# Seven tiny loads on the scalar queue during the last store of a top-2 dispatch kernel

## The chip, the cores and the metric

The kernel runs on one core of a Trainium2 chip. The metric is device time in microseconds (us): the median of several executions. A single profiled execution is shown beside it, because its trace is what can be read. The core has a vector engine (VectorE, DVE in the profile), a scalar engine (ScalarE, ACT), GpSimd (POOL), a matrix engine (TensorE, PE, which has no work here), a sync engine (SyncE, SP) that issues most transfers, and 16 DMA engines that carry the transfers out.

## The reference, cut to what matters

The inputs are `x` with 16 x 1024 tokens of 512 float32 values, and `router_logits` with 8 float32 values for each token. For each token the two largest of the 8 logits are turned into two weights that add up to one, and the token's row of `x` is written out twice, once times each weight.

```python
probs = softmax(router_logits)                     # 8 experts
topk_indices = np.argsort(probs, axis=-1)[..., -k:]  # k = 2, smaller one first
topk_probs = np.take_along_axis(probs, topk_indices, axis=-1)
topk_probs = topk_probs / np.sum(topk_probs, axis=-1, keepdims=True)
x_expanded = x[:, :, np.newaxis, :].repeat(k, axis=2)
return (x_expanded * topk_probs[..., np.newaxis]).astype(np.float32)
```

The output, 16 x 1024 x 2 x 512 float32, is twice the size of `x`. The profile counts 34.08 MB read and 67.11 MB written.

## The kernel before, in words

**Tiling.** The 16,384 tokens are cut into two groups (`GROUPS`, line 42): 65 x 128 tokens, then 63 x 128. In each group every one of the 128 partitions of SBUF holds 65 (or 63) tokens that follow each other in memory, so a transfer of n tokens per partition is 128 long rows, one for each partition. `xs` (line 93) holds a whole group of `x`, `osp` (line 94) is a second buffer of 18 tokens' outputs.

**The weights.** All logits are loaded at the start by two transfers (lines 130 and 131) into a corner of `osp`. `top2_weights` (line 14) finds the two largest by a tournament of maxima and minima on VectorE, and two sigmoids on ScalarE (lines 37 and 38) give the weights `WA`.

**Loads, products, stores.** For each group, `LOADS` (line 44) lists the load sizes in tokens per partition, issued at line 122 on the sync queue, and `STORES` (line 47) lists the stores. For each store VectorE makes the products (line 138), in `osp` or back into parts of `xs` that are no longer needed, and one transfer writes them out (line 151). All stores go over the sync queue but the very first (3 tokens per partition), which goes over the scalar queue (line 149). The stores of the second group are 16, 16, 15 and 16 tokens per partition; the last one is 64 KB for each partition, 8 MB in all.

**The order.** `keep_in_program_order` fixes the order of the transfers on their queue as the loops write it. The list `moved` collects the loads of `x` and all stores in that order, so `moved[-1]` is the last store and `moved[-2]` the one before it. Waits are set by the framework: whoever reads or overwrites a buffer waits for the semaphore of whoever wrote or read it. Eight semaphores go round among the transfers.

**The end.** At line 155 the sync engine gets an empty instruction, `seen`, that waits for the weights, the last product and all transfers of `moved` but the last. What is left for the program's end (line 195 in the profile) is then the wait for the last store alone, and a barrier of all engines.

Of the kernel before, what the change touches and what calls it, by code (L numbers as in the profile page):

```python
# [1 line left out]

# [4 lines left out]

F32 = mybir.dt.float32
ALU = mybir.AluOpType
ACTF = mybir.ActivationFunctionType  # L10
P = 128


def top2_weights(nc, WA, dlt, room, logits, E):

    tt = nc.vector.tensor_tensor
    hi, lo, n = None, None, E  # L20
    while n > 1:
        n //= 2
        if hi is None:
            a, b = logits[:, :, 0:n], logits[:, :, n : 2 * n]
            nhi, nlo = room(n), b
            tt(nhi, a, b, op=ALU.max)  # L26
            tt(nlo, a, b, op=ALU.min)  # L27
        else:
            a, b = hi[:, :, 0:n], hi[:, :, n : 2 * n]
            nhi, nlo, tmp = room(n), room(n), room(n)  # L30
            tt(tmp, lo[:, :, 0:n], lo[:, :, n : 2 * n], op=ALU.max)  # L31
            tt(nlo, a, b, op=ALU.min)  # L32
            tt(nlo, nlo, tmp, op=ALU.max)  # L33
            tt(nhi, a, b, op=ALU.max)  # L34
        hi, lo = nhi, nlo
    tt(dlt, hi[:, :, 0], lo[:, :, 0], op=ALU.subtract)  # L36
    nc.scalar.activation(WA[:, :, 0], dlt, ACTF.Sigmoid, scale=-1.0)  # L37
    return nc.scalar.activation(WA[:, :, 1], dlt, ACTF.Sigmoid, scale=1.0)  # L38

GROUPS = [65, 63]

LOADS = [[2, 4, 28, 31], [16, 16, 31]]
BASE = [0, 1]

STORES = [
    [(0, 3, "osp", 0), (3, 15, "osp", 3), (18, 16, "xs", 0), (34, 15, "osp", 0), (49, 16, "xs", 33)],
    [(0, 16, "osp", 2), (16, 16, "xs", 0), (32, 15, "osp", 0), (47, 16, "xs", 32)],
]  # L50

L = 18

FREE = [3, 2]


@with_exitstack
def kernel(
    ctx: ExitStack,
    tc: tile.TileContext,  # L60
    x: bass.AP,
    router_logits: bass.AP,
    k: bass.AP,
    out: bass.AP,
):
    nc = tc.nc
    B, S, D = x.shape
    E = router_logits.shape[-1]
    N = B * S
    assert int(k) == 2 and E == 8 and N == P * sum(GROUPS)  # L70
    M = N // P

    x_v, o_v, rl_v = [], [], []
    t0 = 0
    for n in GROUPS:
        t1 = t0 + P * n
        x_v.append(
            x.rearrange("b s d -> (b s) d")[t0:t1].rearrange("(p m) d -> p m d", p=P)
        )
        o_v.append(  # L80
            out.rearrange("b s k d -> (b s) k d")[t0:t1].rearrange(
                "(p m) k d -> p m k d", p=P
            )
        )
        rl_v.append(
            router_logits.rearrange("b s e -> (b s) e")[t0:t1].rearrange(
                "(p m) e -> p m e", p=P
            )
        )
        t0 = t1  # L90

    wpool = ctx.enter_context(tc.tile_pool(name="wpool", bufs=1))
    xs = wpool.tile([P, max(GROUPS), D], F32)
    osp = wpool.tile([P, L, 2, D], F32)
    WA = wpool.tile([P, M, 2], F32)
    dlt = wpool.tile([P, M], F32)


    flat = osp.rearrange("p l k d -> p (l k d)")
    taken = [0]  # L100

    def room(n):
        o = taken[0]
        taken[0] += M * n
        return flat[:, o : o + M * n].rearrange("p (m n) -> p m n", n=n)

    logits = room(E)

    def place(where, at, n):

        if where == "osp":
            return osp[:, at : at + n]
        return xs[:, at : at + 2 * n, :].rearrange("p (r k) d -> p r k d", k=2)

    moved = []
    m0 = 0
    for g, G in enumerate(GROUPS):
        x0, r = BASE[g], 0
        for n in LOADS[g]:
            moved.append(  # L120
                tc.keep_in_program_order(
                    nc.sync.dma_start(  # L122
                        xs[:, x0 + r : x0 + r + n, :], x_v[g][:, r : r + n, :]
                    )
                )
            )
            r += n
            if g == 0 and r == 6:
                n0 = GROUPS[0]
                tc.keep_in_program_order(nc.sync.dma_start(logits[:, :n0], rl_v[0]))  # L130
                tc.keep_in_program_order(nc.sync.dma_start(logits[:, n0:], rl_v[1]))  # L131
                weights = top2_weights(nc, WA, dlt, room, logits, E)
        assert r == G
        for r, n, where, at in STORES[g]:
            og = place(where, at, n)
            again = where == "osp" and at == 0 and r > 0
            for a, b in [(0, FREE[g]), (FREE[g], n)] if again else [(0, n)]:
                product = nc.vector.tensor_tensor(  # L138
                    og[:, a:b],
                    xs[:, x0 + r + a : x0 + r + b, :]  # L140
                    .unsqueeze(2)
                    .to_broadcast([P, b - a, 2, D]),
                    WA[:, m0 + r + a : m0 + r + b, :]
                    .unsqueeze(3)
                    .to_broadcast([P, b - a, 2, D]),
                    op=ALU.mult,
                )

            queue = nc.scalar if g == r == 0 else nc.sync
            moved.append(  # L150
                tc.keep_in_program_order(queue.dma_start(o_v[g][:, r : r + n], og))  # L151
            )
        m0 += G

    seen = tc.keep_in_program_order(nc.sync.nop())
    for ins in [weights, product] + moved[:-1]:
        tc.add_manual_dep(
            seen.ins,
            ins.ins.name,
            mybir.DependencyInfo(  # L160
                mybir.DependencyClass.Sync, mybir.DependencyReason.DATA
            ),
            reason="all but the last transfer is done",
        )


# [1 line left out]
_INS = ['x', 'router_logits', 'k']  # L168
_OUTS = [((16, 1024, 2, 512), 'float32')]

_NUMBERS = {'k': 2}


# [26 lines left out]
```

## Time and profile before

| what | value |
|---|---|
| median of 3 runs | 239.66 us (239.65 to 239.67) |
| profiled execution, its own time | 241.36 us |
| span of its trace, first to last instruction | 239.6 us |
| VectorE busy | 141.9 us (59% of the span), 22 instructions |
| ScalarE busy | 1.8 us, 3 instructions |
| data moved | 101.19 MB in 2592 packets, 422 GB/s over the span |

The span is what the profiler recorded between the first and the last instruction; the time of the same execution, 241.36 us, has what lies around the span in it, 1.8 us here. A transfer is recorded twice: as an instruction of the queue that issues it (SPq for sync, ACTq for scalar) and as packets on the 16 DMA engines. Queue q1 is the sync engine's, q10 the scalar engine's. A packet here is one contiguous row of a transfer, or the 4 bytes with which a DMA engine reports on a semaphore that its part is done. The view of a window tells how many packets began in it, and the sum of their durations as a share of 16 engines over the window; a packet that begins in a window counts in full, so the share can be over 100%.

### The profile page before, as it was taken

How to read it: one execution, taken by the hardware profiler on the slowest of the kernel's cores; microseconds unless marked ns; L12 is line 12 of the kernel's file. 1: busy time of each engine (PE TensorE's matmuls, PEld its weight loads, DVE VectorE, ACT ScalarE, POOL GpSimd, SP SyncE). 2: the span in 40 equal slices, each digit the busy share in tenths (PEclk: the TensorE clock that was granted, in tenths of full speed). 3: DMA queues.
4: the chain of work that ended last, by engine and by line, in shares of the span. 5: the costliest groups of instructions: out<-in, count | busy, mean ns of one | idle time of the engine just before them, and what ended most of it. 6: DMA issues, size and time to landing. Idle time of an engine off the chain costs nothing.

```text
span 239.6 us, 106 instructions
## 1 busy us (share of the span) xinstructions
DVE 141.9 (59%) x22; ACT 1.8 (1%) x3; POOL 0.2 (0%) x4
## 2 busy tenths in 40 slices
DVE  0560499999789999200000699999405999960000
ACT  2000000000000000000000000000000000000000
POOL 0000000000000000000000000000000000000000
DMA  7989998979989897999899999999999899898984
GB/s 253 528 373 483 427 415 376 493 339 492 481 372 492 383 482 339 482 437 449 361 421 438 438 438 498 435 419 471 405 405 471 372 503 442 380 492 360 514 350 186
DMA packets 2592, 101.19 MB, mean 422 GB/s; under 512 B 288, under 2 KB 416, under 8 KB 672
## 3 DMA queue, kind: packets, MB, share of 16 engines
q1 hardware_dynamic: 2448, 99.62, 96.7%
q10 hardware_dynamic: 144, 1.57, 1.5%
HBM read 34.08 MB, written 67.11 MB: 422 GB/s over the span
## 4 chain that ended last, share of the span: by engine, by line
DMA 48%; DVE 40%; SPq 1%; issue 0%; DVEq 0%
DMA xs<-in_x_dram 25%; DVE osp L138 25%; DMA out_dram<-osp 23%; DVE xs L138 14%; SPq L122 0%; SPq L131 0%; SPq L130 0%; SPq L151 0%; DVEq L138 0%
## 5 line engine op out<-in xcount | busy, mean ns | idle before, releaser
L138 DVE TENSOR_TENSOR osp<-xs,WA 128x3072 f32<-128x3072 f32 (+5 forms) x7 | 69.4, 9909 | 62.7 <-DMA xs<-in_x_dram 47.3
L138 DVE TENSOR_TENSOR xs<-xs,WA 128x16384 f32<-128x16384 f32 x4 | 68.9, 17224 | 0.1
L26 DVE TENSOR_TENSOR osp<-osp 128x512 f32<-128x512 f32 x1 | 0.7, 693 | 8.5 <-DMA osp<-in_router_logits_dram 8.5
L37 ACT ACT_TABLE_LOAD x1 | 1.3, 1283 | 0.7 <-PEq L181 0.7
L27 DVE TENSOR_TENSOR osp<-osp 128x512 f32<-128x512 f32 x1 | 0.7, 691 | 0.0
L32 DVE TENSOR_TENSOR osp<-osp 128x256 f32<-128x256 f32 (+1 forms) x2 | 0.7, 351 | 0.0
L31 DVE TENSOR_TENSOR osp<-osp 128x256 f32<-128x256 f32 (+1 forms) x2 | 0.7, 350 | 0.0
L34 DVE TENSOR_TENSOR osp<-osp 128x256 f32<-128x256 f32 (+1 forms) x2 | 0.7, 350 | 0.0
L33 DVE TENSOR_TENSOR osp<-osp 128x256 f32<-128x256 f32 (+1 forms) x2 | 0.7, 350 | 0.0
L37 ACT ACTIVATE WA<-dlt 128x128 f32<-128x128 f32 x1 | 0.3, 315 | 10.5 <-DVE dlt L36 10.5
L36 DVE TENSOR_TENSOR dlt<-osp 128x128 f32<-128x128 f32 x1 | 0.3, 292 | 0.0
L38 ACT ACTIVATE WA<-dlt 128x128 f32<-128x128 f32 x1 | 0.3, 297 | 0.0
L181 POOL MEMSET const-bfloat16-1.0<- 128x1 bf16 x1 | 0.1, 101 | 0.0
L181 POOL MEMSET const-uint8-127<- 128x1 uint8 x1 | 0.1, 101 | 0.0
L181 POOL MEMSET const-float32-0.0<- 128x1 f32 x1 | 0.1, 98 | 0.2 <-issue 0.2
L181 POOL MEMSET const-float32-1.0<- 128x1 f32 x1 | 0.1, 98 | 0.0
## 6 DMA issues: line engine op xcount, KB each, us to landing
out_dram<-osp SPq DMA_DIRECT2D x3, 7680.0 KB, 23.5
xs<-in_x_dram SPq DMA_DIRECT2D x2, 7936.0 KB, 42.2
xs<-in_x_dram SPq DMA_DIRECT2D x2, 4096.0 KB, 40.1
xs<-in_x_dram SPq DMA_DIRECT2D x1, 7168.0 KB, 24.8
out_dram<-osp ACTq DMA_DIRECT2D x1, 1536.0 KB, 26.6
xs<-in_x_dram SPq DMA_DIRECT2D x1, 1024.0 KB, 5.9
xs<-in_x_dram SPq DMA_DIRECT2D x1, 512.0 KB, 3.9
osp<-in_router_logits_dram SPq DMA_DIRECT2D x1, 260.0 KB, 6.2
```

Of the source, the lines that this page charges most:

```text
L26: tt(nhi, a, b, op=ALU.max)
L27: tt(nlo, a, b, op=ALU.min)
L31: tt(tmp, lo[:, :, 0:n], lo[:, :, n : 2 * n], op=ALU.max)
L32: tt(nlo, a, b, op=ALU.min)
L33: tt(nlo, nlo, tmp, op=ALU.max)
L34: tt(nhi, a, b, op=ALU.max)
L36: tt(dlt, hi[:, :, 0], lo[:, :, 0], op=ALU.subtract)
L37: nc.scalar.activation(WA[:, :, 0], dlt, ACTF.Sigmoid, scale=-1.0)
L38: return nc.scalar.activation(WA[:, :, 1], dlt, ACTF.Sigmoid, scale=1.0)
L138: product = nc.vector.tensor_tensor(og[:, a:b], xs[:, x0 + r + a : x0 + r + b, :] .unsqueeze(2) .to_broadcast([P, b - a, 2, D]), WA[:, m0 ...
L181: nc = _bacc.Bacc("TRN2", target_bir_lowering=False, num_devices=1)
```

## The change

Behind the two groups' loops, seven small loads are issued on the scalar queue. Load i takes n rows, n = 2, 4, 6, 8, 10, 12, 14, each of 16 + i float32 values (64 to 88 bytes), from the logits into a buffer `marks` that nothing reads. Each is made to wait for `moved[-2]`, the last store but one. They are put at the front of `moved`, so that `seen` waits for them too. The rest of the hunk only gives the dependency a name (`done`).

```diff
+ENGINES = [2, 4, 6, 8, 10, 12, 14]
...
+    marks = wpool.tile([P, len(ENGINES), 16 + len(ENGINES)], F32)
...
+    done = mybir.DependencyInfo(mybir.DependencyClass.Sync, mybir.DependencyReason.DATA)
+    rows = router_logits.rearrange("b s e -> (b s) e").rearrange("(p m) e -> p (m e)", p=P)
+    last = moved[-2]
+    for i, n in enumerate(ENGINES):
+        small = tc.keep_in_program_order(
+            nc.scalar.dma_start(marks[:n, i, : 16 + i], rows[:n, : 16 + i])
+        )
+        tc.add_manual_dep(small.ins, last.ins.name, done, reason="late in the program")
+        moved.insert(0, small)
+
     seen = tc.keep_in_program_order(nc.sync.nop())
     for ins in [weights, product] + moved[:-1]:
         tc.add_manual_dep(
-            seen.ins,
-            ins.ins.name,
-            mybir.DependencyInfo(
-                mybir.DependencyClass.Sync, mybir.DependencyReason.DATA
-            ),
-            reason="all but the last transfer is done",
+            seen.ins, ins.ins.name, done, reason="all but the last transfer is done"
         )
```

In the built program the instructions of all engines but ACT are the same as before, in the same order. ACT has the seven transfers behind its one store; the first six of them wait for semaphores of earlier transfers (the first for two, one of them that of `moved[-2]`), the seventh for none of its own. The names and sizes of the waits of `seen` are unchanged, only the counts that it waits for are higher.

## The prediction

> **What bounds the kernel now.** I read the queues first, then the chain, then the waits of the sync engine, and last the packets in windows at the end. The page's queue part and the chain of waits (start, duration, what, in us):
>
> ```profile
> DMA packets 2592, 101.19 MB, mean 422 GB/s; under 512 B 288, under 2 KB 416, under 8 KB 672
> q1 hardware_dynamic: 2448, 99.62, 96.7%
> q10 hardware_dynamic: 144, 1.57, 1.5%
> ...
> 150.83 31.23 DMA out_dram<-osp
> ...
> 196.15 17.23 DVE xs L138
> ```
>
> The packets fill 96.7 + 1.5 = 98.2% of what 16 engines have in the span: the DMA engines bound the kernel, and whatever adds engine time adds to the end. The packets count out: the 18 transfers have 128 rows each, 18 x (128 + 16) = 2592, and 18 x 16 = 288 are under 512 B. So a transfer puts 8 rows and one tiny packet, its report to a semaphore, on each engine. The tail is the last store. In order of time from the sync queue, its waits (total, times, longest) and the instructions of lines 155 and 195 (ns min/median/max, first and last start):
>
> ```profile
> 213.40 0.33 SPq L151 DMA_DIRECT2D out_dram<-xs  x1
> ...
> out_dram<-xs SPq DMA_DIRECT2D x1, 25.4
> ...
> SPq L195 <- DMA out_dram<-xs: 19.2, 1, 19.2
> SPq L155 <- DMA out_dram<-osp: 5.5, 1, 5.5
> ...
> L155 SPq EVENT_SEMAPHORE  x5: 17/28/5505, 213.8 to 214.0; - x5
> ...
> L195 SPq DRAIN  x3: 7/7/7, 238.8 to 239.1; - x3
> ...
> L195 SPq COMPARE_BRANCH  x1: 33/33/33, 219.6 to 219.6; - x1
> ```
>
> The last store is issued at 213.40 and lands 25.4 later, at 238.8, where the closing drain starts; 0.8 us of barrier follow to 239.6. `seen` at L155 starts the last of its five waits at 214.0 and is held 5.5 us, to 219.5: that is when the last store but one has landed, and when the seven loads may go. Now the end itself, by packets that began in three windows, 236.3 to 237, 236.96 to 238.4, and 238.4 to 239:
>
> ```profile
> DMA packets 15, 0.00 MB, mean 0 GB/s; under 512 B 15, under 2 KB 15, under 8 KB 15
> ...
> q1 hardware_dynamic: 15, 0.00, 1.2%
> ```
>
> ```profile
> DMA packets 0, 0.00 MB, mean 0 GB/s; under 512 B 0, under 2 KB 0, under 8 KB 0
> ```
>
> ```profile
> DMA packets 1, 0.00 MB, mean 0 GB/s; under 512 B 1, under 2 KB 1, under 8 KB 1
> ```
>
> Fifteen engines report by 236.96, the sixteenth after 238.4. So one engine alone sets the end, at least 1.44 us behind the rest. An engine that is not this one has 1.44 us to give away; the late one has nothing. The trace doesn't number the engines, so it doesn't say which of them is late. The 15 reports took 1.2% of 16 x 0.7 us, 0.13 us, or 9 ns each.
>
> **The change part by part.** *Nothing is removed.* Up to 219.5 us no engine has a new instruction, so all before stands as it is, and the 8 MB of the last store are issued at 213.40 as before.
>
> *Issue.* ACT gets seven transfers. Its one transfer before and its one wait:
>
> ```profile
> L151 ACTq EVENT_SEMAPHORE  x1: 38/38/38, 12.5 to 12.5; - x1
> L151 ACTq DMA_DIRECT2D out_dram<-osp x1: 367/367/367, 16.4 to 16.4; - x1
> ```
>
> Seven times 0.37 is 2.6 us, and a few waits of 0.04: ACT issues from 219.5 to about 222.3 and then goes to the closing barrier, which it needs only at 238.8. Queued behind the waiting ACT are only its own seven loads and the barrier. Cover 16.5 us; cost nothing.
>
> *How the packets mix.* Queue q10 has run beside q1 once, with the first store. The window 16.4 to 43:
>
> ```profile
> DMA packets 320, 11.43 MB, mean 430 GB/s; under 512 B 32, under 2 KB 32, under 8 KB 32
> ...
> q1 hardware_dynamic: 176, 9.86, 87.3%
> q10 hardware_dynamic: 144, 1.57, 13.9%
> ...
> out_dram<-osp ACTq DMA_DIRECT2D x1, 1536.0 KB, 26.6
> ```
>
> 1.5 MB took 26.6 us to land although their packets are 13.9% of the engines' time: 9 packets an engine on q10, 11 on q1, about one for one. The shares add to 101.2%, so the mixing itself lost no engine time. I take from it that an engine serves one packet of each queue in turn. Beside the last store a turn is long. The window 221.7 to 236 has only its rows:
>
> ```profile
> DMA packets 95, 6.23 MB, mean 435 GB/s; under 512 B 0, under 2 KB 0, under 8 KB 0
> ...
> q1 hardware_dynamic: 95, 6.23, 100.4%
> ```
>
> 100.4% of 16 x 14.3 us over 95 packets is 2.42 us each. Between about 220.5 and 237 that gives 6 or 7 turns, so 6 or 7 tiny packets an engine slip between rows of the store, and what is left of an engine's tiny packets runs when its store is done. How many an engine gets no row shows for fewer than 128 rows. As 128 rows give 8 to each of 16, I take at most one row per load, so at most 7 rows and 7 reports, 14 packets; the other end is all 56 rows and 7 reports on one engine, 63.
>
> *Price of a tiny packet.* A report of 4 B took 9 ns. The next larger rows are those of the logits, window 7.1 to 7.3, and for the two large rows that also began in it, window 11.5 to 13:
>
> ```profile
> DMA packets 46, 0.20 MB, mean 978 GB/s; under 512 B 4, under 2 KB 41, under 8 KB 44
> ...
> q1 hardware_dynamic: 46, 0.20, 236.2%
> ```
>
> ```profile
> DMA packets 15, 0.86 MB, mean 573 GB/s; under 512 B 0, under 2 KB 0, under 8 KB 0
> ...
> q1 hardware_dynamic: 15, 0.86, 132.2%
> ```
>
> The second gives 1.322 x 24 / 15 = 2.115 us for a 57 KB row. The first is 2.362 x 3.2 = 7.56 us; less two such rows and four reports, 40 rows of about 2 KB share 3.29, or 82 ns each. A row of 64 to 88 B lies between 9 and 82 ns; by size it is close to the report, some 12 ns. Fourteen packets are then 7 x 12 + 7 x 9 = 0.15 us (14 x 82 = 1.15 at the other price; 63 x 12 = 0.76 if all fell on one engine). On fifteen engines that hides in the 1.44 us; on the late one it adds 0.15 at most if it carries a row of every load, and nothing if it carries none. I take 0.05.
>
> *A read between writes.* This is the cost that could be large: the last store only writes to HBM, and each tiny load is a read that ends with a switch back to writing. The nearest rows are the ends of big loads where a store comes next. First the last row of the late engine before a store (window 159.1 to 159.3) and the row before it (156.75 to 156.95), then the same two for the other fifteen (157.8 to 158.6, 155.4 to 156.2):
>
> ```profile
> q1 hardware_dynamic: 1, 0.06, 100.8%
> ...
> q1 hardware_dynamic: 1, 0.06, 73.2%
> ```
>
> ```profile
> q1 hardware_dynamic: 15, 0.95, 279.0%
> ...
> q1 hardware_dynamic: 15, 0.95, 274.5%
> ```
>
> Late engine: 1.008 x 3.2 = 3.23 against 0.732 x 3.2 = 2.34, so 0.88 us more. The fifteen: 2.790 x 12.8 / 15 = 2.38 against 2.34, so 0.04 each. At the end of the 57 KB rows, window 23.0 to 23.9, the row of q1:
>
> ```profile
> q1 hardware_dynamic: 15, 0.86, 264.7%
> ```
>
> 2.647 x 14.4 / 15 = 2.54 against 2.115: 0.43 us more. So a load's last row that is followed by a store has cost 0.04 to 0.88 us more than its size. Against that stands the mixture above: there rows of loads and stores alternated for some 20 us and the shares came to 101.2%, no loss to be seen. Bounds 0 and 0.88 for each tiny load. I take 0, as a load of 64 B has a whole turn of 2.42 us in which its data can be fetched, and the exposed ends were those of 57 to 62 KB.
>
> On this point the Trainium skill speaks against the change: "DMA: Bandwidth & Descriptors", section "Latency and other measured facts", gives HBM access as 0.2 us on average and 2 us at high load. If nothing hid it, three or four reads between the store's rows would by that be an estimated 0.6 to 8 us on an engine; no row here shows a bare read at this load, and the rows above stop at 0.88.
>
> *The wait of `seen`.* It now also holds for the tiny loads. If they land before 238.8, that is nothing. If they land later, the rest of its five waits (213.8 to 214.0, some 0.06 us each) and the branch of 33 ns come behind the end: up to 0.3 us.
>
> Sum: the profiled span of 239.6 plus 0.05, and 241.36 plus 0.05 for the execution; the median, 1.7 below that execution, moves by the same: 239.66 + 0.05, so 239.7.
>
> The skill also bears on who is late: the same page says that engines 7 and 15 are usually the slower ones (same section), and that a transfer of n rows runs on the lowest-numbered engines, n of them for each n here ("Why a DMA increments its semaphore by 16 and not by 1"). By that the late engine would carry none (15) or four loads (7), an estimated 0 or 0.08 us; the trace shows one late engine, not two, and no number for it.
>
> **The rivals.**
>
> *Exposed reads (slower).* Tiny rows and their reports take turns, so 3 or 4 rows fall between rows of the store. If each exposes its read by 0.43 us, a late engine that carries them ends 3.5 x 0.43 = 1.5 us later: 241.2; at 0.88 each, 242.7. One such row on it: 240.1 to 240.5. If it carries none, the others' 1.5 to 3.1 us less 1.44 leave 0.1 to 1.7: 239.8 to 241.4. It decides from 0.5 us on the late engine or 1.9 us on another. For it: the 0.88 and 0.43. Against: 0.04 on fifteen engines, and the mixture without loss. Chance 0.18, of which 0.15 lies over the 0.2%.
>
> *Tiny loads trail the store.* On an engine with 14 tiny packets 7 or 8 are left over after the store. If these come one by one with a wait for memory instead of 12 ns, `seen` is what ends last. The first loads of the kernel show rows that were not fetched ahead, window 1.7 to 3:
>
> ```profile
> DMA packets 59, 0.24 MB, mean 186 GB/s; under 512 B 0, under 2 KB 0, under 8 KB 59
> ...
> q1 hardware_dynamic: 59, 0.24, 88.0%
> ```
>
> 0.88 x 20.8 / 59 = 0.31 us a row. Three or four left over are 0.9 to 1.2 us: hidden by the 1.44 on another engine, but on the late one they and up to 0.3 of `seen` give 240.9 to 241.2; two or fewer give 239.9 to 240.3. The same would come of loads that were held until the store is through, the case in which the change doesn't do what its words say; the window 16.4 to 43 speaks against that. Chance 0.09, half of it over the 0.2%.
>
> *Faster.* The late engine could gain only if its rows ran faster with its neighbours held up a little. The most is the 1.44 us by which it trails: 238.2. Against it: all rows of the store take 2.42 us, with 16 engines at work, and no byte is taken from it. Chance 0.03.
>
> **How the numbers follow.** The forecast, no effect beyond some tenths of a us, has 0.70. A difference of 0.2%, 0.48 us, is about what a measurement of this kernel can tell from no change. Within it: 0.70 + 0.03 of the exposed reads + 0.05 of the trailing = 0.78, less 0.01 for what I have not thought of; slower 0.15 + 0.04 + 0.01 = 0.20; faster 0.03 less 0.01, so 0.02. Predicted: 239.7. The range goes from 239.5 to 241.0: the lower end is the spread of a run that is not changed, the upper takes in a few exposed rows and a trailing load; what lies above is the dearer half of the exposed reads.
>
> **What would show it.** Right: the last store is issued at 213.4 and lands at 238.8 to 239.0; q10 has 56 packets of 64 to 88 B and their reports more than before, and an end window in which one engine reports 1.3 us or more behind the next. The share of the window 221.7 to 236 stays near 100%, with the same number of store rows within a few. Wrong: fewer store rows in that window, or tiny packets of 0.2 us and more, which would be exposed reads; the closing drain no longer held by the last store but `seen` by the tiny loads, which would be trailing; a last report before 238.4, which would be the gain that I don't see.

## The result and the profile after

The median rose from 239.66 to 240.48 us (240.34 to 240.83, 5 runs; before 239.48 to 240.15, 5 runs). The ratio is 1.0033, with a 95% interval of 1.0019 to 1.0048: 0.5 to 1.2 us slower. The same kernel once more (e11) gave 1.0018 (1.0003 to 1.0032). The time lies in the stated range, but the likeliest case, no effect, is not what happened.

The profiled execution of after ran 240.54 us with a span of 238.8. A transfer has landed when the last of its reports has counted on its semaphore. The queue part, and the last store's time from issue to landing:

```profile
span 238.8 us, 114 instructions
...
DMA packets 2704, 101.19 MB, mean 424 GB/s; under 512 B 400, under 2 KB 528, under 8 KB 784
...
q1 hardware_dynamic: 2448, 99.62, 97.0%
q10 hardware_dynamic: 256, 1.58, 1.6%
```

```profile
out_dram<-xs SPq DMA_DIRECT2D x1, 25.4
```

The span is *shorter* than in the profile of before (239.6) although the kernel is slower. That is the first thing to explain, and the answer is in the other profile: the execution of before that was profiled took 241.36 us, 1.7 more than its own median, and this one sits at its median. The new packets are 112: 56 rows and 56 reports, so each row brought one report, one row to an engine. Next, the windows 235.9 to 236.95 and 236.95 to 239, the waits of the sync queue, and the instructions of `seen` (now line 168) and of the end (now line 203):

```profile
DMA packets 69, 0.00 MB, mean 2 GB/s; under 512 B 69, under 2 KB 69, under 8 KB 69
...
q10 hardware_dynamic: 53, 0.00, 3.3%
q1 hardware_dynamic: 16, 0.00, 0.9%
```

```profile
DMA packets 0, 0.00 MB, mean 0 GB/s; under 512 B 0, under 2 KB 0, under 8 KB 0
```

```profile
SPq L168 <- DMA marks<-in_router_logits_dram: 25.2, 3, 24.6
```

```profile
L168 SPq EVENT_SEMAPHORE  x5: 17/28/125, 236.8 to 237.7; - x5
...
L203 SPq DRAIN  x3: 7/7/7, 238.0 to 238.3; - x3
L203 SPq EVENT_SEMAPHORE  x2: 17/17/17, 238.2 to 238.7; - x2
L203 SPq COMPARE_BRANCH  x1: 33/33/33, 237.9 to 237.9; - x1
```

All 16 engines report for the store by 236.95 here; none is late. The store was issued at 211.84 and landed 25.4 later, at 237.2. Before, the closing drain started when the store landed (238.8 and 238.8). Here it starts at 238.0, 0.8 us behind the store, because `seen` is still waiting: it was held 25.2 us by the tiny loads. Yet no packet begins after 236.95. The 53 tiny packets of q10 at the end took 3.3% of 16 x 1.05 us, 10 ns each. So the engines were done with the tiny loads' packets 0.3 us *before* the store counted as landed, and still the last loads landed after it: the last wait of `seen` starts at 237.7 and ends 0.125 us later, at 237.8. The time is not in the packets but in the landings.

### The profile page after: what moved, and what is told of

It reads as the page before. It is cut to its first block, busy times and chain, and to the rows that moved or that the text cites. A ratio compares the mean times of both kernels' runs of the same rounds, so it can differ in the third digit from the quotient of the medians.

```text
span 238.8 us, 114 instructions
## 1 busy us (share of the span) xinstructions
DVE 141.9 (59%) x22; ACT 1.8 (1%) x3; POOL 0.2 (0%) x4
## 4 chain that ended last, share of the span: by engine, by line
DMA 48%; DVE 40%; SPq 1%; issue 0%; DVEq 0%
DVE osp L141 25%; DMA xs<-in_x_dram 25%; DMA out_dram<-osp 22%; DVE xs L141 14%; SPq L125 0%; SPq L134 0%; SPq L133 0%; SPq L154 0%; DVEq L141 0%
```

## The experiments

The runs from e1 on are set against the kernel before with a median of 240.03 us (240.02 for e9 to e11). Its executions run from 239.54 to 241.63 us, so ratios with their intervals are used. Three theories stood: *trailing* (what lands behind the store is waited for), *exposed reads* (a read between the store's rows stops the engine), and a *fixed price* of having such loads.

**e1, the kernel before once more.** No edit.

> The kernel before, unchanged. Trailing theory: in an ordinary execution no DMA engine reports 1.4 us behind the next; the profile of before was 1.7 us above the median because of that one engine, so a new profile has a span near 237.9 us and its last reports within 0.6 us of each other. Rival (the late engine is always there, and the tiny loads cost by exposed reads): the span is again near 239.6 us with one engine 1.4 us late. Time: 239.66 by both.

239.96 us against 240.03, ratio 0.9995 (0.9985 to 1.0006). The new profile has a span of 238.1 us. The packets that began from 236.2 to 237, those from 237 to 239, and the closing drain:

```profile
DMA packets 16, 0.00 MB, mean 0 GB/s; under 512 B 16, under 2 KB 16, under 8 KB 16
```

```profile
DMA packets 0, 0.00 MB, mean 0 GB/s; under 512 B 0, under 2 KB 0, under 8 KB 0
```

```profile
out_dram<-xs SPq DMA_DIRECT2D x1, 25.4
```

```profile
L195 SPq DRAIN  x3: 7/7/7, 237.3 to 237.6; - x3
```

All sixteen reports stand within 0.8 us, and the drain starts at 237.3, where the store (issued at 211.92) has landed. The 1.44 us by which one engine trailed in the first profile belonged to that execution, not to the kernel. The same showed again in e2, where one engine reported after 237.9 and none from 236.95 to 237.9, and in e7, where one of sixteen reported after 237.5. Those two profiled executions took 240.82 and 241.67 us, each 0.8 more than the median of its own kernel (240.03 and 240.89).

**e2, three loads that fit.**

```diff
-ENGINES = [2, 4, 6, 8, 10, 12, 14]
+ENGINES = [16, 16, 16]
```

> Only three tiny loads, of 16 rows each, so that every engine has at most 6 tiny packets, which fit into the 6 or 7 turns left beside the last store. Trailing theory: the loads land before the store does, the closing drain is held by the store alone, 239.66 us, no change (below 239.9). Exposed reads: three reads between the store's rows on every engine, 0.1 to 1.3 us more, and fewer store rows in the same window. A fixed price of having such loads at all (semaphores, program, issue): about three sevenths of 0.82, so 240.0 us.

240.03 us, ratio 1.0004 (0.9987 to 1.002): no change. The three loads' size and time to landing, and what held the closing drain:

```profile
marks<-in_router_logits_dram ACTq DMA_DIRECT2D x1, 1.0 KB, 8.6
marks<-in_router_logits_dram ACTq DMA_DIRECT2D x1, 1.1 KB, 13.0
marks<-in_router_logits_dram ACTq DMA_DIRECT2D x1, 1.1 KB, 16.8
```

```profile
SPq L203 <- DMA out_dram<-xs: 0.7, 1, 0.7
```

The loads were issued at 218.98, 219.35 and 220.38, so they landed at 227.6, 232.4 and 237.2, 4.8 us apart: two packets on each engine for each load, one turn of 2.4 us for each packet. That is the one-for-one mixture of the prediction, measured. They land ahead of the store, and the drain waits for the store again.

Two things keep this run from saying more. Its interval, up to 0.2%, still holds the 0.15% (0.35 us) that a fixed price would be here; it is e5 that decides on that. And the profiled execution is the one with the late engine:

```profile
q1 hardware_dynamic: 1, 0.00, 0.1%
...
L203 SPq COMPARE_BRANCH  x1: 33/33/33, 237.5 to 237.5; - x1
```

The one report after 237.9 is that engine's. `seen` is through at 237.5, and the drain was held for only 0.7 us more, the time by which this engine trailed. So the zero of this trace doesn't say what an execution without a late engine has. e6 below begins with the same three loads and has no late engine: there the third lands at 219.25 + 17.6 = 236.8, 0.3 us ahead of the store. As 0.5 us pass in e7 from the last load's landing to the drain, some 0.2 us would be left behind the store, an estimate. The three loads only just fit.

**e3, the seven loads earlier.**

```diff
-    last = moved[-2]
+    last = moved[-4]
```

> The seven loads of the change, but the first waits for moved[-4] instead of moved[-2]; the loads start some 38 us earlier, beside the two stores before the last. All 14 tiny packets of an engine then find a turn before the last store ends. Trailing theory: 239.66 us, no change. Exposed reads: the same reads between store rows, so the same 240.5 us or more. Fixed price: 240.5 us.

241.5 us, ratio 1.0064 (1.0051 to 1.0077): slower than the change; only exposed reads had left room for that. The trace shows another cause. The sync queue's waits, and its last two stores:

```profile
SPq L154 <- DMA out_dram<-xs: 32.1, 1, 32.1
```

```profile
199.88 0.33 SPq L154 DMA_DIRECT2D out_dram<-osp  x1
211.86 0.33 SPq L154 DMA_DIRECT2D out_dram<-xs  x1
```

The last store but one is issued at 199.88; in after it was issued at 194.59. It waits for an earlier store, 32.1 us. The eight semaphores go round in the order of the program; seven loads more ahead of this store gave it the semaphore of a store that was still under way, and it had to wait until that was free. From 198 to 203 us the DMA share fell to 0.47; in e1 it was 0.91 in the same window:

```profile
198.00:203.00 5.00, 5.00 (x1) 0.00 (x0) 0.00 (x0) 1.00 0.47 197
```

The run tells nothing on the theories. It was repeated without that wait as e5.

**e4, seven loads of two rows.**

```diff
-ENGINES = [2, 4, 6, 8, 10, 12, 14]
+ENGINES = [2, 2, 2, 2, 2, 2, 2]
```

> Seven loads of 2 rows each instead of 2 to 14: 14 rows in place of 56, but the engines that carry them have as many tiny packets (14) as the fullest in the change. Trailing theory: the leftovers of two engines are enough to end last, so 240.2 to 240.5 us. A price by rows or by packets in all: a quarter of 0.82, so 239.9 us. Exposed reads: 240.4 if the two engines' reads cost, but then store rows are missing on two engines only.

240.35 us, ratio 1.0022 (1.0012 to 1.0033). Fourteen rows on two engines cost 0.3 to 0.8 us. A price by rows in all would have been a quarter of the change's, 0.2 us or 0.09%, just below the interval's 0.12%. The store was issued at 211.76 and landed 25.4 later, at 237.2; the drain starts at 237.6:

```profile
SPq L168 <- DMA marks<-in_router_logits_dram: 24.7, 2, 22.2
```

```profile
L168 SPq EVENT_SEMAPHORE  x5: 17/28/124, 234.3 to 237.3; - x5
...
L203 SPq DRAIN  x3: 7/7/7, 237.6 to 237.9; - x3
```

**e5, early and with an eighth load.**

```diff
-ENGINES = [2, 4, 6, 8, 10, 12, 14]
+ENGINES = [2, 4, 6, 8, 10, 12, 14, 14]
...
-    last = moved[-2]
+    last = moved[-4]
```

> As e3 the first load waits for moved[-4], but with an eighth load of 14 rows, so that the semaphores come out another way and the last two stores wait for tiny loads that landed long before, and not for a big store. 63 to 70 tiny rows go between store rows, 16 packets on the fullest engines, and none is left at the end. Trailing theory: no change against before (within 0.1%). Exposed reads: eight reads on the fullest engines between store rows, 0.3 to 3.5 us more.

239.94 us, ratio 0.9998 (0.9983 to 1.0012): no change. With 70 tiny rows beside the last stores, the window 183 to 235 and the wait of the end:

```profile
DMA packets 524, 22.55 MB, mean 434 GB/s; under 512 B 172, under 2 KB 172, under 8 KB 172
...
q1 hardware_dynamic: 384, 22.54, 100.0%
q10 hardware_dynamic: 140, 0.01, 0.2%
```

```profile
SPq L203 <- DMA out_dram<-xs: 19.2, 1, 19.2
```

The stores' rows fill 100.0% of the engines while 140 tiny packets pass between them, and the end is held by the store alone: it was issued at 211.96, and the drain starts at 237.4. That ends the theory of exposed reads, whose least was 0.3 us here (0.125%), just outside the interval. It also ends the fixed price: eight loads at a seventh of 0.82 us each would be 0.9 us, 0.39%. The change's own trace says the same: from 221.7 to 236 its q1 and that of e1 have an equal line.

```profile
q1 hardware_dynamic: 96, 6.29, 101.5%
```

**e6, seven loads of 16 rows.** `ENGINES = [16] * 7`, no other edit.

> Seven loads of 16 rows: 14 packets on every engine, so the last engine to end its store rows is sure to carry leftovers, four reports of them. Reports theory (each trailing load lands 0.18 us after the one before): last landing 0.55 to 0.75 us behind the store's and 0.2 us of waits, so 0.3 to 0.4% more than before, as the change. A price by rows in all (112 instead of 56): 0.7% more.

240.8 us, ratio 1.0038 (1.0016 to 1.0059). Twice the rows of the change at a ratio like the change's; a price by rows (0.7%) is outside the interval. The store landed at 237.1 (211.66 + 25.4), the drain starts at 238.0. The landings of the fourth and the seventh load, and the drain:

```profile
marks<-in_router_logits_dram ACTq DMA_DIRECT2D x1, 1.2 KB, 16.9
...
marks<-in_router_logits_dram ACTq DMA_DIRECT2D x1, 1.4 KB, 14.1
...
L203 SPq DRAIN  x3: 7/7/7, 238.0 to 238.3; - x3
```

The fourth was issued at 220.36 and landed at 237.3, the seventh at 223.68 and landed at 237.8: three more landings in 0.5 us, 0.17 us each.

**e7, three loads of 112 rows.** `ENGINES = [112, 112, 112]`.

> Three loads of 112 rows: 7 rows and one report on each engine per load, 24 packets, some 17 of them left over when the store is through, but only three reports. Reports theory: three landings 0.18 us apart behind the store's, some 0.1 us for the packets and 0.2 of waits, 0.3 to 0.6 us in all (0.15 to 0.25% more). A price by leftover packets (7 or 8 of them made 0.8 us in the change): 1.7 us, 0.7% more. Exposed reads: 6 or 7 rows between the store's rows on all engines, 0.25 to 6 us more.

240.89 us, ratio 1.0037 (1.0022 to 1.0052). This is above the reports theory's 0.15 to 0.25%, though the interval reaches down to it, and below 0.7%. What I had left out is where the loads' semaphores stand among the waits of `seen`:

```profile
L168 SPq EVENT_SEMAPHORE  x5: 17/28/28, 238.7 to 238.9; - x5
...
L203 SPq DRAIN  x3: 7/7/7, 239.2 to 239.5; - x3
```

The third load's semaphore is asked for by the first of the five waits. So four waits, the branch and the way to the drain all come behind the last landing: 0.5 us from 238.7 to 239.2, on top of the 0.5 us from the store's landing (212.73 + 25.5 = 238.2) to 238.7. In the change the seventh load's semaphore is asked for last, and only some 0.2 us come behind it (from 237.8 to 238.0).

**e8, the loads left out of `seen`.**

```diff
-        moved.insert(0, small)
```

> The change without putting the seven loads into the list that seen waits for; the program's end waits for them all the same. Trailing theory: the last landing is where it was, 0.5 us behind the store's; what seen's waits cost behind it (0.2 us) is done by the closing waits instead, so 0.3 to 0.4% more than before, as the change, or up to 0.1 us off it. If it were the wait of seen that costs, and not the landings: 239.66, no change.

240.34 us, ratio 1.001 (0.9997 to 1.0022): not told apart from no change, and the change's 0.33% is above its interval. In the trace the tiny loads are now waited for at line 202, by the end's own waits:

```profile
SPq L202 <- DMA marks<-in_router_logits_dram: 19.5, 3, 18.9
```

```profile
L202 SPq DRAIN  x3: 7/7/7, 237.7 to 238.0; - x3
```

The store landed at 237.2 (211.62 + 25.6), the drain starts 0.5 us behind it. So it isn't the wait of `seen` as such that costs, which the ratio alone would allow: the landings are still waited for. But less comes behind them: by the traces' semaphore records the drain starts 0.02 us behind the last tiny load's landing here, and 0.2 us behind it in the change and in e11. Whether that makes the kernel faster is not shown. The distance from the store to the drain is 0.2 to 0.3 us shorter than in the change's first profile and the same as in e11, and the ratios' intervals overlap.

**e9, seven loads of 112 rows, e10, one load of 128, and e11, the change again.** `ENGINES = [112] * 7`, `ENGINES = [128]`, and no edit.

> Seven loads of 112 rows: 56 packets on each engine, of which some 49 with all seven reports are left over when the store is through. Reports theory: seven landings 0.17 us apart, 1.2 us behind the store's, and 0.2 us of waits: 1.3 to 1.6 us more than before (0.55 to 0.7%). If a trailing load cost by its rows as well, 42 rows of 12 ns add 0.5 us and it would be 1.9 to 2.1 us (0.8 to 0.9%). If the price were one for trailing at all, however many: 0.8 us (0.33%).

> One load of 128 rows: 8 rows and one report on each engine, so two or three packets are left over, one of them a report. Reports theory: one landing 0.17 us behind the store's and some 0.3 us for the waits of seen that come behind that one and for the drain: 0.4 to 0.55 us (0.15 to 0.25%). One price for trailing at all: 0.8 us (0.33%). No price for a single load: 0.

> The changed kernel once more, on the same chip as e9 and e10. Reports theory: 0.6 to 0.9 us more than before (0.25 to 0.38%), between e10 and e9, with its seventh load landing about 0.5 us behind the store.

e9: 241.78 us, ratio 1.0071 (1.0052 to 1.009). e10: 240.54 us, ratio 1.0016 (1.0 to 1.0031). e11: 240.46 us, ratio 1.0018 (1.0003 to 1.0032). e10 is where the reports theory put it (0.15 to 0.25%), and one price for trailing at all (0.33%) lies just outside its interval. e9's interval holds the reports theory's 0.55 to 0.7% and a price by rows as well (0.8 to 0.9%), so the trace has to decide. e11 came out under the expected 0.25 to 0.38%, with an interval that reaches into it; its store landed at 211.87 + 25.4 = 237.3 and its last wait of `seen` ends at 237.6, so the last load trails by 0.3 us, not by the 0.5 that were expected:

```profile
L168 SPq EVENT_SEMAPHORE  x5: 17/28/125, 234.5 to 237.5; - x5
...
L203 SPq DRAIN  x3: 7/7/7, 237.8 to 238.1; - x3
```

In e9 all seven reports of an engine are left over. The packets of 235.9 to 237.8 and of 237.75 to 239.8, the issue of the seven loads, the first and the last load's landing, and the end:

```profile
DMA packets 830, 0.05 MB, mean 29 GB/s; under 512 B 830, under 2 KB 830, under 8 KB 830
...
q10 hardware_dynamic: 814, 0.05, 30.9%
```

```profile
DMA packets 0, 0.00 MB, mean 0 GB/s; under 512 B 0, under 2 KB 0, under 8 KB 0
```

```profile
L163 ACTq DMA_DIRECT2D marks<-in_router_logits_dram x7: 338/1014/1074, 218.3 to 224.0; - x7
```

```profile
marks<-in_router_logits_dram ACTq DMA_DIRECT2D x1, 7.0 KB, 19.5
...
marks<-in_router_logits_dram ACTq DMA_DIRECT2D x1, 9.6 KB, 14.9
```

```profile
L203 SPq DRAIN  x3: 7/7/7, 239.1 to 239.4; - x3
```

No packet begins after 237.75. The store landed at 212.21 + 25.5 = 237.7, the first load at 218.34 + 19.5 = 237.8, the seventh at 223.98 + 14.9 = 238.9. Six more landings took 1.04 us, 0.17 us each, while the 814 tiny packets took 30.9% of 16 x 1.9 us, 11.5 ns each. e9 puts seven rows of a load between two reports of an engine, e6 one, and the landings are 0.17 us apart in both. So the landings that trail queue up one behind the other at 0.17 to 0.18 us, whatever their rows. In e10 the one load landed at 218.0 + 19.5 = 237.5, 0.1 to 0.2 us behind the store (211.86 + 25.5 = 237.4), and the drain starts at 237.8.

From the store's landing to the closing drain, by the traces (to 0.1 us), beside the measured ratio:

| kernel | reports that trail on the fullest engine | store lands to drain, us | ratio (95%) |
|---|---|---|---|
| before (e1) | 0 | 0.0 | 0.9995 (0.9985 to 1.0006) |
| e5, eight early | 0 | 0.0 | 0.9998 (0.9983 to 1.0012) |
| e2, three of 16 | 0 | 0.0, with a late engine | 1.0004 (0.9987 to 1.002) |
| e10, one of 128 | 1 | 0.5 | 1.0016 (1.0 to 1.0031) |
| e4, seven of 2 | 4 | 0.5 | 1.0022 (1.0012 to 1.0033) |
| e11, the change again | 4 | 0.5 | 1.0018 (1.0003 to 1.0032) |
| e8, not in `seen` | 4 | 0.5 | 1.001 (0.9997 to 1.0022) |
| the change | 4 | 0.8 | 1.0033 (1.0019 to 1.0048) |
| e7, three of 112 | 3 | 1.0 | 1.0037 (1.0022 to 1.0052) |
| e6, seven of 16 | 4 | 0.9 | 1.0038 (1.0016 to 1.0059) |
| e9, seven of 112 | 7 | 1.4 | 1.0071 (1.0052 to 1.009) |

The count of reports is an estimate from the turns: two packets for each load, or more, and 6 or 7 turns beside the store. In us, each distance lies in its ratio's interval, e8's at the upper end of it. The price is the time from the store's landing to the drain, and it is made of landings of 0.17 to 0.18 us and of the waits that come behind the last one. Why a landing takes that long, no run shows.

It isn't the count alone: e4 and e6 have four each and 0.5 against 0.9 us. The waits of `seen` tell why, as each goes on when its load has landed (by the traces' records of these five waits). In e6 the last four go on at 237.29, 237.46, 237.63 and 237.80, all behind the store's landing at 237.1. In e4 they go on at 236.89, 237.07, 237.25 and 237.43, just as far apart, but the first of them 0.2 us before the store's last report: the two engines that carry its loads were not the last to end their store rows. The change has both cases: its last two waits go on at 237.65 and 237.84 in the first profile, and at 237.44 and 237.63 in e11, with the store landing at 237.3 in both. So what counts is how much the engine that ends last still carries, and for the change that differed between its two profiles.

## Where the prediction held and where it failed, point by point

**The range and the number.** 240.48 us lies between 239.5 and 241.0, but that is no merit of the mechanism that was forecast. The forecast was 239.7, with 0.70 for no effect. The upper end was set for "a few exposed rows and a trailing load", two rivals with 0.18 and 0.09, and the time lies between the two cases of the trailing one (239.9 to 240.3, and 240.9 to 241.2). The three chances, 0.77 after its deduction, 0.20 and 0.02, add up to 0.99; nothing hangs on it.

**What bounds the kernel, issue time and mixture: mostly right.** The DMA engines bound it, nothing changed before the loads, and an engine does serve one packet of each queue in turn: e2's loads land 4.8 us apart, two turns of 2.4. Rows of 64 to 88 B took some 12 ns and left the store's rows at full rate (e5). ACT's issue was priced too low: the seven took 495 to 919 ns each, not 370, 6 us instead of 2.6. It is hidden, as the loads wait for turns anyway.

```profile
L163 ACTq DMA_DIRECT2D marks<-in_router_logits_dram x7: 495/911/919, 218.0 to 223.0; - x7
```

**The step that failed: "Fifteen engines report by 236.96, the sixteenth after 238.4 ... An engine that is not this one has 1.44 us to give away."** That was read from one execution and taken as the kernel's. In e1 the cover is not there, and all engines end within 0.8 us. It could have been seen: the profiled execution took 241.36 us, and the median was 239.66. I wrote down this gap of 1.7 us and let the sum go on with "moves by the same". A gap of that size beside a spread of 239.65 to 239.67 says that the profile holds something that the timed runs don't, and a single late engine of 1.44 us was the candidate on the page.

**The wait of `seen`: mechanism seen, size wrong, chance wrong.** "If they land later, the rest of its five waits ... come behind the end: up to 0.3 us." The rest cost 0.2 to 0.5 us (the change and e11, e7). The rival *Tiny loads trail the store* is what happened; it had 0.09, because the late engine seemed to hide it on all others.

**Its price came from the wrong thing.** In the sum, the seven reports of an engine stood at 7 x 9 = 63 ns, and in the rival I charged 0.31 us for each row that isn't fetched ahead. The rows took 12 ns; it was each *report* that took 0.17 to 0.18 us to land. So without the late engine's cover the sum would still have been too low. The Trainium skill names a rule of this shape: in "DMA: Bandwidth & Descriptors", section "Queues, rings and completion order", the write to the semaphore is strongly ordered and lands only after every earlier write of that engine, on all of its queues. e9 agrees in so far as the landings come in a row behind the store's, 0.17 us apart, when no packet is left to move. That the ordering itself makes the 0.17 us is not shown; no run separates it from another cost of a landing.

**Exposed reads and a gain: both fell.** e5 gives a ratio of 0.9998 with 70 reads between store rows. The extra 0.43 to 0.88 us at the ends of big loads are not a price of a switch from reading to writing as such. The Trainium skill's 0.2 us on average and 2 us at high load for HBM access ("Latency and other measured facts", same page), by the prediction an estimated 0.6 to 8 us if nothing hid it, do not show up as added time: e5 carries eight reads on the fullest engines at no measurable cost.

**Who is late.** That engines 7 and 15 are usually slower, which the prediction took from the Trainium skill, can't be judged, as the trace doesn't number them. The prediction left out that the section's own best guess at the cause, not certain by its words, lies with transfers that GpSimd issues; this kernel's two queues are those of sync and scalar. What the traces show is that one late engine is there in some executions (the first profile, e2, e7) and not in others (e1, after).

## What to carry to other kernels

Before an argument leans on slack in a profile, compare the profiled execution's own time with the median: where it is higher by about the slack, as in three profiles here, the slack is likely that execution's. A small transfer beside a large one costs a turn for each of its packets, so count packets against turns; what has not landed when the large one is through is waited for, and here that cost 0.17 to 0.18 us for each report and next to nothing for its rows. Work that must only be done "by the end" belongs early enough to land ahead of the last transfer, and the waits that are satisfied last belong last in the list.

## What the runs showed that I had not expected

- A transfer of few rows took longer to issue than one of 128: 0.50 us for the first of the change's seven, 0.91 us at the median, against 0.33 to 0.37 us for a store of 128 rows. In e9, with 112 rows each, the first took 0.34 and the median 1.01, so it isn't only the number of rows; loads that follow each other closely take longer. Why stays open.
- Landings that are left over come 0.17 to 0.18 us apart though their packets take 9 to 12 ns.
- An added transfer can move another one by the semaphore that it takes from the round: e3's last store but one was issued 5.3 us later (199.88 against 194.59), and the kernel was 0.5 to 0.8% slower.
